# Four small edits ahead of the first layer's convolution output: halo copies, one norm's squares, the sums for a mean, and the start of the modulation columns

## Chip, cores and metric

The kernel runs on one core of one Trainium2 chip. The metric is the device time of one execution in microseconds; the time before is the median of three runs. The profile is that of one execution, with times counted from its span's start. The engines are called as in the profile: PE (matrix products), DVE (vector), ACT (scalar activation), POOL (GpSimd), SP (whose queue issues most transfers).

## The reference, cut to what matters

Sequence 1024, width 1024, two layers, batch 1, everything in float32. Only the first half of layer 0 is touched by the change:

```python
mod = c_act @ ada_w[i] + ada_b[i]
sh_m, sc_m, g_m, sh_f, sc_f, g_f = jnp.split(mod, N_ADA, axis=-1)
h = modulate(rms_norm(x, norm_mix_g[i]), sh_m, sc_m)
u = h @ w1 + b1                       # D -> 2D
a, g = jnp.split(u, 2, axis=-1)
u = a * jax.nn.sigmoid(g)
u = causal_depthwise_conv(u, w_dw, width=31) + b_dw
u = jax.nn.silu(layer_norm(u, ln_g, ln_b))
x = x + (1.0 + g_m) * (u @ w2 + b2)
```

After it come a SwiGLU feed-forward net (width 2816), and in layer 1 a pooling mixer and a second such net, then a last norm.

## The kernel before

The work lies transposed: channels on the 128 partitions, time along the free axis. There are eight channel tiles (`KT`, called k or p) and two chunks of 512 time steps, A and B. A float32 product is made as three products of 512 columns (`products`): every matrix and every activation is split in a high and a low part, and high by high, high by low and low by high are added in one PSUM bank. `matmul` (line 119) is the one place that issues on PE, so all of PE's instructions have line 122; the `Engine` helper issues all of DVE's, ACT's and POOL's, at line 100.

**Order.** PE's instructions run in the order in which the program emits them. The other engines' orders are laid out by a scheduler at build time, from modelled times and priorities, and are then fixed: each engine and each queue runs its list in order and waits at the head of it. What is emitted when is set by a planner: `unit` collects the stages; `run_units` emits them one after the other; `pace()` (called after each fourth k of a product, and at the end of each unit) lets background tasks emit as much as the planner's clocks of PE, DVE and POOL allow. `finish` and `need` force a task to its end before the next unit. A task that says "load", "stats" or "spread" is left alone for 2.5, 2.75 or 1.5 us of the planner's clock.

**Weights.** `load_weight` (line 394) reads a 512 KB tile to a `raw` buffer (three of them) from SP's queue at line 397; ACT makes the high part (line 399) and the negated high part (line 401); a second read of the same tile, issued by POOL at line 403, adds itself to the latter, which gives the low part. There are five buffers for the pair of parts (`W_BUFS`).

**Stages around the change**, in PE's order: the products of the first four channel pairs of chunk A (tiles `first`); `conv_in((A, 4))` and `conv_in((A, 5))`, each 24 products of `a` and 24 of `g`; then pairs 6 and 7 of A and, with the same weights, of B; pairs 0, 1 and 2 of B; the depthwise convolution of channel tile 7 of chunk A as products with diagonal matrices (`pe_taps`, tile `tap`); pairs 3 and 4 of B; the product with w2 for chunk A (`conv_out`, tile `y`).

**Background tasks** beside them:
- `ada_columns` (line 352) makes four of layer 0's six modulation vectors (j = 2 to 5). For each j there are eight steps; each loads a 512 KB tile `adaw` (two buffers, SP's queue, line 132), and PE takes it in a group of four short products into a bank `ada`. After the eighth step `columns_done` copies the bank (ACT), turns it into columns with four tiny products (bank `adac`), and adds the bias. The task is started by the unit `ada_first` (line 1041), ahead of `conv_in((A, 4))`. A unit after `pe_taps` forces it to its end (line 1065); vectors that end after `held` is set wait for `conv_out`.
- `norm_first` (line 1045) is the norm of chunk B: `Squares.add(k)` squares a tile on ACT and adds it on DVE to a sum in a PSUM bank; then mean, reciprocal root (`mean_rsqrt`: products `var`, twelve small DVE instructions, products `rstd`) and modulation to the tiles `hhi`, `hlo`. It is forced to its end ahead of pair 6 of chunk B.
- `Taps` does the other seven channel tiles' depthwise convolution of chunk A: 31 taps each, on DVE (`ca`, sums in the two spare PSUM banks) or on ACT and POOL (`pr`, `pa`), joined at the end.
- `layer_norm_silu(A)` (line 703) adds the eight convolved tiles up on DVE as they are ready (`acc`), makes the `mean` on PE, subtracts it, and goes on to squares, `var`, `rstd` and the tiles `vhi`, `vlo` that `conv_out` needs.

`conv_glu` (line 562) makes u from `a` and `g`, and for chunk A copies u's last 30 columns to `uhalo` on POOL (line 568), from where `conv_u` copies them in front of chunk B's u, on POOL as well. `bank` hands out one of six PSUM banks, `temp` one of four SBUF tiles named t, or one of two named `acc`.

Of the kernel before, what the change touches and what calls it, by code (L numbers as in the profile page):

```python
# [12 lines left out]
AF = mybir.ActivationFunctionType  # L13
ALU = mybir.AluOpType
MUL, ADD, SUB = ALU.mult, ALU.add, ALU.subtract
# [4 lines left out]
KT = D // P  # L20
# [4 lines left out]
HALO = CW - 1  # L25
# [15 lines left out]
FIRST = 4  # L41
# [64 lines left out]
def trunk(ctx, tc, xT, c, vec, ada, adan, w1, w2, wgu, wdn, wpl, out):  # L106
# [3 lines left out]
    V_ = Engine(nc.vector, "V", clock, PRICES["V"], lambda i: order(i))  # L110
    G_ = Engine(nc.gpsimd, "G", clock, PRICES["G"], lambda i: order(i))
    S_ = Engine(nc.scalar, "S", clock, PRICES["S"], lambda i: order(i))
# [11 lines left out]
    def order(ins):  # L124

        if behind[0] and last_mm[0] is not None:
            tc.add_manual_dep(ins.ins, last_mm[0], edge, reason="behind the products")
        return ins
# [29 lines left out]
    def nm(s):  # L158
        uid[0] += 1
        return f"{s}_{uid[0]}"  # L160
# [7 lines left out]
    def step(t, e):  # L168
        behind[0] = not t.urgent
        before = {k: engines[k].spent for k in "VG"}  # L170
        with tc.high_priority(offset=0 if t.urgent else -LATER):
            moved = t.step(e)
        behind[0] = False
        for k in "VG":
            clock[k] += (stretch[0] - 1) * (engines[k].spent - before[k])
        return moved
# [13 lines left out]
    def finish(*these):  # L190
        forced[0] = True
        for t in these:
            while not t.done:
                e = "V" if clock["V"] <= clock["G"] else "G"
                o = "VG"[e == "V"]
                if not any(step(q, e) for q in [t] + tasks) and not any(step(q, o) for q in [t] + tasks):
                    raise RuntimeError("nothing moves")
                clock["PE"] = max(clock["PE"], min(clock["V"], clock["G"]))
        forced[0] = False

    class Task:


        def __init__(self, gen, urgent=False, at=None):
            self.gen, self.done, self.urgent, self.until, self.mark = gen, False, urgent, 0.0, None
            tasks.insert(0 if urgent else len(tasks) if at is None else at, self)
# [31 lines left out]
    def bank(name):  # L238
        return ps.tile([P, 512], F32, tag="mm", name=nm(name))
# [15 lines left out]
    def temp(n, name="t", bufs=0):  # L255
        t = tmp.tile([P, TMPW], F32, tag=name if bufs else "t", name=nm(name), bufs=bufs or 4)
        return t[:, :n]
# [9 lines left out]
    x = [[cst.tile([P, ch.n], F32, name=f"x_{ch.i}_{k}") for k in range(KT)] for ch in chunks]  # L267
# [21 lines left out]
    def V(name, j, n=1):  # L289
        b = _COLS[name] + j  # L290
        return vecs[:, b : b + n]
# [4 lines left out]
    uhalo = cst.tile([P, KT, HALO], F32, name="uhalo")  # L296
# [158 lines left out]
    class Squares:  # L455


        def __init__(self, ch, psum=False):
            self.ch, self.acc, self.psum = ch, None, psum

        def add(self, k):
            ch = self.ch
            if self.acc is None:
                self.acc = bank("acc") if self.psum else temp(ch.n, "acc", 2)
                S_.activation(self.acc, x[ch.i][k], AF.Square)
            else:
                sq = temp(ch.n)
                S_.activation(sq, x[ch.i][k], AF.Square)
                was = self.acc
                if self.psum and k == KT - 1:  # L470
                    self.acc = temp(ch.n, "acc", 2)
                V_.tensor_tensor(self.acc, was, sq, op=ADD)

    def sum_sq(srcs, n):
        acc = None
# [50 lines left out]
    def unit(emit, *weights):  # L526
        units.append((weights, emit))
# [26 lines left out]
    def conv_u(ch, p):  # L554
        u = st["u", ch.i, p] = wslot(ch, "u")
        if ch.i == 0:
            G_.memset(u[:, :HALO], 0.0)
        else:
            G_.tensor_copy(u[:, :HALO], uhalo[:, p, :])
        return u  # L560

    def conv_glu(ch, p, ba, bg):
        u = st["u", ch.i, p]
        sg = temp(ch.n)
        S_.activation(sg, bg, AF.Sigmoid, bias=V("conv_b1", KT + p))
        V_.scalar_tensor_tensor(u[:, HALO:], ba, V("conv_b1", p), sg, op0=ADD, op1=MUL)
        if ch.i == 0:
            G_.tensor_copy(uhalo[:, p, :], u[:, ch.n : ch.n + HALO])

    def conv_in(*todo):  # L570

        def emit(take):
            got = {}
            for each in todo:
                if each is None:
                    finish(T["norm_b"])
                    continue
                ch, p = each
                conv_u(ch, p)
                wts = got.setdefault(p, [])  # L580
                b = [bank("a"), bank("g")]
                for i in range(2):
                    if len(wts) == i:
                        wts.append(take())
                    for k in range(KT):
                        products(b[i], wts[i], k, st["h", ch.i][k], k == 0, k == KT - 1)
                        if k % 4 == 3:
                            pace()
                conv_glu(ch, p, *b)
                if ch.i == 0 and p in PE_TAPS:  # L590
                    split_u(p)
                elif ch.i == 0:
                    T["taps", 0, p] = Taps(A, p)
        tiles = list(dict.fromkeys(e[1] for e in todo if e))
        unit(emit, *[w1[p, i] for p in tiles for i in range(2)])

    def split_u(p):

        u = st["u", 0, p]
        hi, lo = st["us", p] = [wslot(B, name, F32R) for name in ("uhi", "ulo")]  # L600
        S_.copy(hi, u)
        either(A.width).tensor_tensor(lo, u, hi.bitcast(F32), op=SUB)
# [100 lines left out]
    def layer_norm_silu(ch):  # L703

        n = ch.n
        vs = [st["u", ch.i, k][:, HALO:] for k in range(KT)]
        acc = temp(n, "acc", 2)
        for k in range(1, KT):
            while not (st["taps", ch.i][k - 1] and st["taps", ch.i][k]):
                yield "wait"  # L710
            V_.tensor_tensor(acc, vs[0] if k == 1 else acc, vs[k], op=ADD)
            yield
        yield "stats"
        b = bank("mean")
        matmul(b, ones, acc, start=True, stop=True)
        if ch.i == 0:
            yield from centred(vs, b, n)
        else:
            for k in range(KT):
                V_.tensor_tensor(vs[k], vs[k], b, op=SUB)  # L720
                yield
        acc = yield from sum_sq([vs[k] for k in CENTRED], n)
        rstd = yield from mean_rsqrt(acc, n)
        S_.activation(tmp.tile([P, 16], F32, tag="col0", name=nm("col"), bufs=1)[:, 0:1], acc[:, 0:1], AF.Silu)
        hv = [(slot(ch, "vhi"), slot(ch, "vlo")) for _ in range(KT)]
        for k in range(KT):
            V_.tensor_tensor(vs[k], vs[k], rstd, op=MUL)
            sw = temp(n)
            S_.activation(sw, vs[k], AF.Silu, bias=V("conv_ln_b", k), scale=V("conv_ln_g", k))
            hi, lo = hv[k]  # L730
            if ch.i == 0 and k % 2 == 0:
                V_.tensor_copy(hi, sw)
            else:
                S_.copy(hi, sw)
            (either(n) if ch.i else (G_, V_)[k % 2]).tensor_tensor(lo, sw, hi.bitcast(F32), op=SUB)
            yield
        st["v", ch.i] = hv
# [222 lines left out]
    acc = now(sum_sq([x[0][k] for k in range(KT)], A.n))  # L960
# [52 lines left out]
    T = {}  # L1013
# [6 lines left out]
    def need(*names):  # L1020
        unit(lambda take: finish(*(T[n] for n in names)))
# [19 lines left out]
    def ada_first(take):  # L1041
        T["ada", 0] = Task(ada_columns((2, 3, 4, 5)), False, 0)
        T["ada", 0].free = True
    unit(ada_first)
    def norm_first():
        squares = Squares(B, True)
        for k in range(KT):
            squares.add(k)
            yield
        yield from norm(B, 0, False, ("h", 1), squares=squares)  # L1050
    unit(lambda take: T.__setitem__("norm_b", Task(norm_first(), False, 0)))
    taps(A, *range(FIRST))
    for p in range(FIRST, KT - 1 - SHARE):
        conv_in((A, p))
    some = range(KT - 1 - SHARE, KT)
    conv_in(*[(A, p) for p in some], None, *[(B, p) for p in some])
    put("ln_a", lambda: layer_norm_silu(A), True)
# [4 lines left out]
        for u in pe_taps(p):  # L1062
            unit(*u)
    unit(lambda take: held.__setitem__(0, True))
    unit(lambda take: finish(T["ada", 0]))
    unit(lambda take: finish(*(T["taps", 0, p] for p in range(KT) if p not in PE_TAPS)))
    for p in rest[len(rest) - HOLD - HOLD_LN : len(rest) - HOLD]:
        conv_in((B, p))
    need("ln_a")
    sq_a = Squares(A)  # L1070
    conv_out(A, sq_a, lambda take: [now(columns_done(*g)) for g in held_back])
# [49 lines left out]
    fb_, fa_, last = ffn(B, 0, True), ffn(A, 1, True), ffn(B, 1, True, at_end=True)  # L1121
# [51 lines left out]
```

## Time and profile before

| what | value |
|---|---|
| time, median of three runs | 1880.17 us (1877.83 to 1882.66) |
| the profiled execution's own time | 1878.38 us |
| its span | 1876.6 us |
| busy: PE, DVE, ACT, POOL | 1821.7, 971.8, 984.5, 622.2 us |
| mean clock granted to PE | 0.989 |
| PE waits on `adaw` transfers | 10.4 us in 6 waits |

A group's row reads: line, engine, operation, tile written and tiles read, shapes and count; busy time and mean duration in ns; and, behind the second bar, how long the engine stood idle ahead of the group and what ended that. A row of the timeline reads: start, time that it took, engine, line, operation, tiles, count, and in brackets the idle time before it with its releaser. Rows that begin with SPq or POOLq, or that have line 397 or 403, are transfers; their time is that of issuing, not of moving data. PE's matrix products overlap, so its rows show the time of one product (some 0.39 us) while a new one starts every 0.227 us.

### The profile page before, as it was taken

The page shows a single profiled execution, that of the slowest core. Times are in us where ns is not written, and L with a number is a line of the kernel's source. Part 1 is how long each engine was busy: PE and PEld are TensorE (multiplying, and loading weights), DVE is VectorE, ACT ScalarE, POOL GpSimd, SP SyncE. Part 2 cuts the span into 40 slices and gives each one's busy share as a digit, 9 for nine tenths or more (in the row PEclk, how much of TensorE's full clock was granted, in tenths as well). Part 3 has the DMA queues.
Part 4 walks back from the last instruction along what each step waited for, and adds up shares of the span by engine and source line. Part 5 has one row for each costly group of instructions (what it writes and reads, how often), then busy time and mean ns, then how long its engine had stood idle before and what let it go on. Part 6 is the DMA issues. An engine that isn't in the chain of part 4 may idle for free.

```text
span 1876.6 us, 22033 instructions
## 1 busy us (share of the span) xinstructions
PE 1821.7 (97%) x8197; PEld 1481.9 (79%) x8197; DVE 971.8 (52%) x1489; ACT 984.5 (52%) x1304; POOL 622.2 (33%) x668
## 2 busy tenths in 40 slices
PE   6899999999999999999999999999999999999996
PEld 4676678888888887888888888888888888888886
DVE  7699743998876235486533223644432233323225
ACT  3577756866756454554553445645534454443443
POOL 3488621787753211273211111421111111111111
PEclk9999989999999999999999999999999999999998
DMA  8968558899897986999887887878878879788882
GB/s 265 298 185 233 155 114 202 207 230 218 213 233 186 239 217 165 261 266 291 231 204 181 200 197 179 196 180 208 185 181 199 198 174 247 180 206 187 193 185 61
DMA packets 115292, 382.31 MB, mean 204 GB/s; under 512 B 11889, under 2 KB 22257, under 8 KB 115186
## 3 DMA queue, kind: packets, MB, share of 16 engines
q0 software_dynamic: 43488, 158.35, 46.2%
q1 hardware_dynamic: 70544, 221.51, 34.8%
q8 instruction: 64, 1.05, 0.2%
q10 hardware_dynamic: 1154, 1.05, 0.2%
q14 instruction: 42, 0.34, 0.0%
HBM read 376.67 MB, written 4.19 MB: 203 GB/s over the span
## 4 chain that ended last, share of the span: by engine, by line
PE 91%; DVE 4%; DMA 3%; ACT 0%; issue 0%; POOL 0%; SPq 0%; DVEq 0%; ACTq 0%; POOLq 0%
PE dn L122 25%; PE gate L122 25%; PE up L122 24%; PE y L122 6%; PE a L122 3%; PE g L122 3%; PE first L122 2%; DMA adaw<-in_adan_dram 2%; DVE t L100 1%; PE ada L122 1%; PE tap L122 1%; DVE x L100 1%; DVE adaw L100 1%; PE var L122 1%; DMA w<-in_wdn_dram 1%; DVE acc L100 1%
## 5 line engine op out<-in xcount | busy, mean ns | idle before, releaser
L100 ACT CAST w<-raw 128x1024 fp32r<-128x1024 f32 x312 | 326.0, 1045 | 514.8 <-issue 294.4
L122 PE MATMUL dn<-ghi,w 128*128 128x512 f32 (+1 forms) x1440 | 450.0, 389 | 2.2 <-ACT ghi L100 1.2
L122 PE MATMUL up<-hhi,w 128*128 128x512 f32 x1408 | 451.4, 390 | 0.0
L122 PE MATMUL gate<-hhi,w 128*128 128x512 f32 x1408 | 450.9, 390 | 0.0
L403 POOL DMA_DIRECT2D w<-in_wgu_dram x176 | 154.2, 876 | 767.6 <-ACT w L100 750.1
L100 DVE SCALAR_TENSOR_TENSOR x<-dn,gains,x 128x512 f32<-128x512 f32 (+1 forms) x360 | 261.8, 735 | 122.1 <-PE dn L122 121.7
L122 PEld LDWEIGHTS dn<-ghi,w 128*128 128x128 f32 x1440 | 270.4, 189 | 62.0 <-ACT ghi L100 1.6
L100 ACT ACTIVATE w<-raw 128x1024 fp32r<-128x1024 f32 x302 | 318.9, 1056 | 0.0
L100 DVE TENSOR_TENSOR t<-t,up 128x512 f32<-128x512 f32 x88 | 60.4, 686 | 492.4 <-PE up L122 472.0
L122 PEld LDWEIGHTS gate<-hhi,w 128*128 128x128 f32 x1408 | 264.3, 188 | 55.4
L122 PEld LDWEIGHTS up<-hhi,w 128*128 128x128 f32 x1408 | 264.3, 188 | 54.7
L122 PE MATMUL dn<-glo,w 128*128 128x512 f32 (+1 forms) x720 | 280.7, 390 | 1.6 <-POOL glo L100 1.6
L122 PE MATMUL gate<-hlo,w 128*128 128x512 f32 x704 | 274.3, 390 | 1.5 <-DVE hlo L100 1.5
L122 PE MATMUL up<-hlo,w 128*128 128x512 f32 x704 | 273.9, 389 | 0.0
L100 POOL TENSOR_TENSOR pa<-pa,pr 128x512 f32<-128x512 f32 x165 | 231.0, 1486 | 23.0 <-ACT pr L100 20.3
L100 DVE SCALAR_TENSOR_TENSOR ca<-u,vecs,ca 128x512 f32<-128x512 f32 x255 | 176.2, 746 | 0.7
L122 PEld LDWEIGHTS dn<-glo,w 128*128 128x128 f32 x720 | 136.6, 190 | 30.3 <-POOL glo L100 1.9
L122 PEld LDWEIGHTS gate<-hlo,w 128*128 128x128 f32 x704 | 132.1, 188 | 29.8 <-DVE hlo L100 2.3
L122 PEld LDWEIGHTS up<-hlo,w 128*128 128x128 f32 x704 | 132.2, 188 | 27.2
L403 POOL DMA_DIRECT2D w<-in_wdn_dram x88 | 77.9, 885 | 226.5 <-ACT w L100 224.4
L100 ACT ACTIVATE t<-gate 128x512 f32<-128x512 f32 x88 | 52.3, 594 | 161.0 <-PE gate L122 154.4
L100 DVE SCALAR_TENSOR_TENSOR adaw<-adaw,cact 128x1024 f32<-128x1024 f32 x64 | 106.2, 1660 | 36.0 <-DMA adaw<-in_ada_dram 35.8
(134 smaller groups left out, 1792.3 us busy)
## 6 DMA issues: line engine op xcount, KB each, us to landing
raw<-in_wgu_dram SPq DMA_DIRECT2D x176, 512.0 KB, 7.2
w<-in_wgu_dram POOLq DMA_DIRECT2D x176, 512.0 KB, 8.0
raw<-in_wdn_dram SPq DMA_DIRECT2D x88, 512.0 KB, 5.4
w<-in_wdn_dram POOLq DMA_DIRECT2D x88, 512.0 KB, 9.1
adaw<-in_ada_dram SPq DMA_DIRECT2D x48, 512.0 KB, 7.8
raw<-in_w_dram SPq DMA_DIRECT2D x44, 512.0 KB, 6.2
w<-in_w_dram POOLq DMA_DIRECT2D x34, 512.0 KB, 8.1
adaw<-in_adan_dram SPq DMA_DIRECT2D x32, 512.0 KB, 5.3
```

Of the source, the lines that this page charges most:

```text
L100: self.last = self.order(getattr(self.eng, name)(out, *args, **kw))
L122: last_mm[0] = nc.tensor.matmul(out, lhsT, rhs, start=start, stop=stop).ins.name
L403: order(nc.gpsimd.dma_start(low if len(src.shape) == 2 else low.rearrange("p (a b) -> p a b", a=src.shape[1]), src, accum_op=ADD))
```

## The change

1. `conv_glu` copies u's last columns to `uhalo` on DVE, not POOL.
2. `Squares` is cut in two, `square(k)` and `sum`, and `norm_first` squares tile k before it adds tile k-1. Elsewhere `add` does what it did.
3. In `layer_norm_silu` the sums for the mean of chunk A go to a PSUM bank, all but the last, which goes to an SBUF tile; for chunk B they stay in SBUF, the last going to a second tile.
4. `ada_first` moves behind `conv_in((A, 4))`, and the unit that forces the task to its end moves behind pairs 3 and 4 of chunk B.

```diff
-        def add(self, k):
+        def square(self, k):
             ch = self.ch
-            if self.acc is None:
-                self.acc = bank("acc") if self.psum else temp(ch.n, "acc", 2)
-                S_.activation(self.acc, x[ch.i][k], AF.Square)
+            if k == 0:
+                self.acc = sq = bank("acc") if self.psum else temp(ch.n, "acc", 2)
             else:
                 sq = temp(ch.n)
-                S_.activation(sq, x[ch.i][k], AF.Square)
-                was = self.acc
-                if self.psum and k == KT - 1:
-                    self.acc = temp(ch.n, "acc", 2)
-                V_.tensor_tensor(self.acc, was, sq, op=ADD)
+                self.waiting.append(sq)
+            S_.activation(sq, x[ch.i][k], AF.Square)
+
+        def sum(self, last):
+            was = self.acc
+            if self.psum and last:
+                self.acc = temp(self.ch.n, "acc", 2)
+            V_.tensor_tensor(self.acc, was, self.waiting.pop(0), op=ADD)
+
+        def add(self, k):
+            self.square(k)
+            if k:
+                self.sum(k == KT - 1)
...
-            G_.tensor_copy(uhalo[:, p, :], u[:, ch.n : ch.n + HALO])
+            V_.tensor_copy(uhalo[:, p, :], u[:, ch.n : ch.n + HALO])
...
-        acc = temp(n, "acc", 2)
+        acc = None
         for k in range(1, KT):
             while not (st["taps", ch.i][k - 1] and st["taps", ch.i][k]):
                 yield "wait"
-            V_.tensor_tensor(acc, vs[0] if k == 1 else acc, vs[k], op=ADD)
+            was = vs[0] if k == 1 else acc
+            if k == KT - 1 or ch.i and acc is None:
+                acc = temp(n, "acc", 2)
+            elif acc is None:
+                acc = bank("acc")
+            V_.tensor_tensor(acc, was, vs[k], op=ADD)
             yield
...
-    unit(ada_first)
     def norm_first():
         squares = Squares(B, True)
-        for k in range(KT):
-            squares.add(k)
+        for k in range(KT + 1):
+            if k < KT:
+                squares.square(k)
+            if k > 1:
+                squares.sum(k == KT)
             yield
         yield from norm(B, 0, False, ("h", 1), squares=squares)
...
         conv_in((A, p))
+        if p == FIRST:
+            unit(ada_first)
...
-    unit(lambda take: finish(T["ada", 0]))
     unit(lambda take: finish(*(T["taps", 0, p] for p in range(KT) if p not in PE_TAPS)))
     for p in rest[len(rest) - HOLD - HOLD_LN : len(rest) - HOLD]:
         conv_in((B, p))
+    unit(lambda take: finish(T["ada", 0]))
     need("ln_a")
```

More of the change, by code (lines that the diff above doesn't have):

```diff
@@ L458, in __init__ @@
         def __init__(self, ch, psum=False):
-            self.ch, self.acc, self.psum = ch, None, psum
-        def add(self, k):
+            self.ch, self.acc, self.psum, self.waiting = ch, None, psum, []
+        def square(self, k):
             ch = self.ch
-            if self.acc is None:
-                self.acc = bank("acc") if self.psum else temp(ch.n, "acc", 2)
-                S_.activation(self.acc, x[ch.i][k], AF.Square)
+            if k == 0:
+                self.acc = sq = bank("acc") if self.psum else temp(ch.n, "acc", 2)
             else:
                 sq = temp(ch.n)
-                S_.activation(sq, x[ch.i][k], AF.Square)
-                was = self.acc
-                if self.psum and k == KT - 1:
-                    self.acc = temp(ch.n, "acc", 2)
-                V_.tensor_tensor(self.acc, was, sq, op=ADD)
+                self.waiting.append(sq)
[9 more added lines that the diff above has]
+                self.sum(k == KT - 1)
     def sum_sq(srcs, n):
```

## The prediction, made before the result was known

> **What bounds the kernel now.** I read the busy time by stage first, to see where PE stands still.
>
> ```profile
> 70.70:93.30 22.60, 15.89 (x82) 10.28 (x80) 11.47 (x17) 14.29 (x21) 9.51 (x12) 0.85 0.99 270
> ...
> 231.50:254.50 23.00, 16.09 (x52) 12.42 (x52) 12.79 (x29) 11.48 (x16) 7.12 (x9) 0.70 0.55 114
> ...
> 338.30:1829.00 1490.70, 1486.94 (x6572) 1225.81 (x6571) 701.76 (x1036) 758.87 (x941) 441.25 (x471) 1.00 0.85 207
> ```
>
> The second and third columns are the stretch's length and PE's busy time; the third from the right is the granted clock. From 338 us on PE idles 3.8 us in 1491, so an edit ahead of 338 us is worth only what it takes out of PE's gaps ahead of 338 us. Two stretches hold most: 6.7 us at 70.7 to 93.3, 6.9 us at 231.5 to 254.5, each with a lowered clock on top. The table of waits names two of the causes:
>
> ```profile
> PE ada L122 <- DMA adaw<-in_adan_dram: 10.4, 6, 6.0
> ...
> PE mean L122 <- DVE acc L100: 4.7, 1, 4.7
> ```
>
> **The first stretch** is `conv_in((A, 4))`. PE's timeline, and one row of the chain that ended last for the length of 24 products:
>
> ```profile
> 70.73 0.39 PE L122 MATMUL a<-hhi,w 128*128 128x512 f32 x1
> ...
> 73.54 0.64 PE L122 MATMUL ada<-adaw,ccols 128*32 128x256 f32 x8
> ...
> 77.06 0.64 PE L122 MATMUL ada<-adaw,ccols 128*32 128x256 f32 x8
> ...
> 86.62 1.08 PE L122 MATMUL ada<-adaw,ccols 128*32 128x256 f32 x8 [5.97 <-DMA adaw<-in_adan_dram]
> ...
> 92.68 0.64 PE L122 MATMUL ada<-adaw,ccols 128*32 128x256 f32 x8 [0.74 <-DMA adaw<-in_adan_dram]
> 93.25 0.50 PE L122 MATMUL a<-hhi,w 128*128 128x512 f32 x1
> ```
> ```profile
> 258.23 5.44 PE a L122 x24
> ```
>
> A product takes 5.44 / 24 = 0.227 us; from one column group to the next, 73.54 to 77.06, are 3.52 us for 12 products (2.72) and a group, so a group costs 0.80. The pair needs 48 x 0.227 + 4 x 0.80 = 14.1 us and took 93.25 - 70.73 = 22.5. Of the 8.4 lost, 6.7 are the two waits on `adaw`, and 1.7 is the halved clock behind the first (its group took 1.08, not 0.64).
>
> **The second stretch** is the layer norm of chunk A:
>
> ```profile
> 236.20 2.08 PE L122 MATMUL mean<-acc,ones 128*128 128x512 f32 x2 [4.66 <-DVE acc L100]
> ...
> 247.56 1.86 PE L122 MATMUL var<-ones,acc 128*128 128x1 f32 x8 [2.25 <-DVE acc L100]
> 249.29 0.77 PE L122 MATMUL g<-hhi,w 128*128 128x512 f32 x1
> ...
> 254.41 1.05 PE L122 MATMUL rstd<-ident,col 128*128 128x128 f32 x8
> ```
> ```profile
> 248.00:252.00 4.00, 4.00 (x14) 3.42 (x15) 2.01 (x12) 0.86 (x2) 0.67 (x1) 0.50 0.75 181
> ```
>
> PE waits 4.66 us for the sums of the mean and 2.25 for those of the squares; the clock is then 0.50, and the 12 products from 249.29 to 254.41 take 5.1 us, not 2.7: 2.4 more.
>
> **Edit 4, the columns' start.** It takes nothing away: 32 loads, 32 groups. All move behind 48 products, 10.9 us of PE. What else moves is SP's queue. Its rows, POOL's first and last of three additive reads, and the page's queues:
>
> ```profile
> 65.94 0.90 SPq L132 DMA_DIRECT2D adaw<-in_adan_dram  x2
> 71.37 2.80 SPq L397 DMA_DIRECT2D raw<-in_w_dram  x2
> 74.28 2.53 SPq L132 DMA_DIRECT2D adaw<-in_adan_dram  x1
> 76.90 0.46 SPq L397 DMA_DIRECT2D raw<-in_w_dram  x1
> 77.76 0.33 SPq L132 DMA_DIRECT2D adaw<-in_adan_dram  x1
> 80.99 0.33 SPq L397 DMA_DIRECT2D raw<-in_w_dram  x1
> ```
> ```profile
> 71.99 1.04 POOL L403 DMA_DIRECT2D w<-in_w_dram  x1 [0.54 <-issue]
> ...
> 76.82 0.86 POOL L403 DMA_DIRECT2D w<-in_w_dram  x1 [1.33 <-issue]
> ```
> ```profile
> q0 software_dynamic: 43488, 158.35, 46.2%
> q1 hardware_dynamic: 70544, 221.51, 34.8%
> ```
>
> Four `adaw` loads leave the time from 66 to 78 us. By the queues' shares of the 1876.6 us span a 0.524 MB additive read occupies all transfer engines for 0.462 x 1876.6 x 0.524 / 158.35 = 2.87 us, a `raw` or `adaw` for 1.55. Pair 4 then runs without a group, 70.73 to 81.6. The first group comes 12 products later, at 84.3. Its load is tied behind pair 4's last product, so it takes SP's queue behind the four `raw` reads up to 80.99, with the three additive reads before it. From 71.4 on that is 4 x 1.55 + 3 x 2.87 + 1.55 = 16.4 us of transfers: it lands at 87.8. PE waits 3.5 us, and the clock costs 1.7 again: 5.2 in place of 8.4. **Gain 3.2.** Bounds: the load in time (8.4), and a load behind everything with no gain (0). I take the middle since the queue's sum says so. The later `adaw` waits (10.4 - 6.7 = 3.7 us) I leave: the columns still run beside pairs 0 to 2 of chunk B, which read fresh weights.
>
> Behind the waiting group stand the other products of pair 5, and the taps of its u; behind its load in SP's queue, the `raw` reads of pair 7 and later, not wanted for 25 us.
>
> ```profile
> 223.04 0.64 PE L122 MATMUL ada<-adaw,ccols 128*32 128x256 f32 x8 [1.20 <-DMA adaw<-in_adan_dram]
> ```
>
> This is the last column group, at the fifth of seven pauses of `pe_taps`. Four pauses later, two fall in the taps and two in pair 3 of chunk B, ahead of `var`. That wait hangs on DVE's sums, not on PE, so 2 x 0.80 = 1.6 us of its 2.25 are filled: **gain 1.6**. Whether the 0.65 us left still halve the clock no row tells; the ends are 0 and 2.4, and I take half, **1.2**.
>
> On this point the Trainium skill ("TensorE: Matmul & The Clock Gate", Part 1: The HAM clock gate) says that the clock halves after an idle window of some 3.4 us. The rows speak against so long a gap: 2.25 us were enough here. By the page the 2.4 would be saved whole, and the sum would be 1.2 lower.
>
> **Edits 1 to 3** work on DVE and POOL:
>
> ```profile
> L100 POOL COPY uhalo<-u x8: 201/208/471, 69.7 to 140.1; 128x30 f32<-128x30 f32 x8
> ```
> ```profile
> L100 DVE TENSOR_TENSOR acc<-acc,u 128x512 f32<-128x512 f32 x6 | 11.1, 1857 | 0.2
> ...
> L100 DVE TENSOR_TENSOR acc<-acc,t 128x512 f32<-128x512 f32 x7 | 4.9, 697 | 0.6
> ```
> ```profile
> 226.71 1.05 ACT L100 CAST w<-raw 128x1024 fp32r<-128x1024 f32 x1 [3.05 <-PE tap L122]
> ...
> 231.77 1.27 POOL L100 TENSOR_TENSOR pa<-pa,pr 128x512 f32<-128x512 f32 x1
> ...
> 233.07 0.70 DVE L100 TENSOR_TENSOR ca<-pa,ca 128x512 f32<-128x512 f32 x1 [6.87 <-POOL pa L100]
> ```
>
> The sums of the mean take 1857 ns each where another sum of that size takes 697. With one input in PSUM six cost at best 6 x 1.16 = 7.0 us less; at worst nothing. The eight copies cost DVE 0.2 us each if they run as on POOL, 1.6 (the taps stand behind them; the far end is the last rival); the squares ahead take short waits out of DVE's list. None of it reaches PE by itself: the mean's wait ends with a chain that begins on PE. A tap product frees a weight buffer (226.7), ACT makes two weight parts ahead of POOL's last factor, POOL ends at 233.0, and DVE, idle for 6.87 us by then, adds it. DVE being 5 us earlier makes that idle time longer. So I cost edits 1 to 3 at **0**; if that chain weren't there, up to the 4.66 us of the mean's wait would go.
>
> **Sum.** 3.2 + 1.6 + 1.2 = 6.0 us from the profiled execution's 1878.4: **1872.4**. That execution lies 1.8 us under the median of 1880.2.
>
> **Rivals.**
>
> *The column comes in time* (0.18). The scheduler may put the load ahead of a `raw` read, or the reads may run faster without it. Then the 5.2 go too, and perhaps the clock's other 1.2: 1866. Against it: SP's queue would have to reach it before 79 us.
>
> *The waits only move* (0.15). The load lands as late after its need as before, or the two groups don't fall ahead of `var`: 1878.
>
> *The sum's bank* (0.17, the slower side). The running sum now sits in one of six banks from the first sum, near 137 us, to the mean. Products take two per pair, the columns one:
>
> ```profile
> 204.56 0.50 PE L122 MATMUL tap<-uhi,diag 128*128 128x512 f32 x1
> ```
> ```profile
> 202.03 0.73 DVE L100 SCALAR_TENSOR_TENSOR u<-a,vecs,t 128x512 f32<-128x512 f32 x1
> ...
> 213.82 0.75 DVE L100 SCALAR_TENSOR_TENSOR u<-a,vecs,t 128x512 f32<-128x512 f32 x1 [0.42 <-ACT t L100]
> ```
>
> DVE frees pair 1's bank at 202.8 and pair 2's at 214.6, PE wants the taps' bank at 204.6. With the sum, a column's bank and four of two pairs all six are held. If the taps' bank must be pair 2's, PE waits 10.0 us, with the clock's 2.4, and as much clock again if pair 2's second bank waits for 202.8: 14.8 more, 1887. It decides from 12 us on. For it speaks how late DVE is with u; against it that pair 1's banks are free 1.8 us before the taps, if the scheduler picks those.
>
> *The copies are dear* (0.05).
>
> ```profile
> 133.05 1.78 DVE L100 SCALAR_TENSOR_TENSOR hlo<-t,mod,hhi 128x512 fp32r<-128x512 f32 x1
> ```
> ```profile
> 135.61 0.50 PE L122 MATMUL a<-hhi,w 128*128 128x512 f32 x1
> ```
> ```profile
> L100 POOL TENSOR_TENSOR pa<-pa,pr 128x512 f32<-128x512 f32 x165 | 231.0, 1486 | 23.0 <-ACT pr L100 20.3
> ```
>
> If each copy waits for a whole POOL sum, 8 x 1.49 = 11.9 us come on DVE ahead of chunk B's `hlo`. The last `hlo` ends at 134.8 and is needed at 135.6 + 21 x 0.227 = 140.4: 5.6 us are hidden, 6.3 are not: 1878.7. The Trainium skill ("SBUF — State Buffer", Who interferes with whom) has this rule: a DVE copy within SBUF in a two-port mode and a GpSimd instruction lock each other out, whichever starts later waiting; it also says that two SBUF inputs on DVE collide with GpSimd's reads, to which the 1857 ns agree.
>
> **How the numbers follow.** The forecast has 0.45, with its own range of 1867 to 1877. A measurement of this kernel tells some 0.3% from no change: 5.6 us, so faster is under 1874.5 and slower over 1885.8. Faster: 0.33 of the forecast and all of the first rival, 0.51. Slower: 0.15, of the banks. The same: 0.34. The range is 1863 (the first rival, with part of the mean's wait gone too) to 1883; it leaves out most of the banks' case and the far end of the first rival.
>
> **What would show it.** In the changed profile the first `ada` group stands in pair 5, 60 products after 70.73; its wait on `adaw` is 2 to 5 us and the only one over 2. Two `ada` groups lie between `mean` and `var`, and `var` waits under 1 us. The rows `acc<-acc,u` of chunk A take some 0.7 us, and the mean still waits 4 to 5 us on a chain through POOL. A PE wait on DVE's u or ACT's t between 137 and 235 us would be the bank. A mean that waits under 2 us would show edits 1 to 3 worth more than nothing; any PE gap over 3 us after 338 us would be a re-laid order that I did not foresee.

## The result, and the profile after

The changed kernel takes 1894.07 us (median of four runs, 1891.56 to 1898.28) against 1879.0 for the kernel before beside it: a ratio of 1.0079, 95% interval 1.0058 to 1.0100. It is slower by some 15 us, where 6 us less were forecast. The profiled execution took 1894.32 us, with a span of 1892.6.

Its table of waits (engine, tile and what PE waited for; us in all, times, longest):

```profile
PE ada L122 <- DMA adaw<-in_adan_dram: 6.3, 5, 1.9
PE mean L122 <- DVE acc L100: 6.1, 1, 6.1
PE adac L122 <- ACT t L100: 5.8, 1, 5.8
...
PE rstd L122 <- DVE uhalo L100: 2.8, 1, 2.8
PE a L122 <- DMA w<-in_w_dram: 2.5, 1, 2.5
...
PE a L122 <- DVE hlo L100: 2.1, 1, 2.1
```

The wait on `adaw` did shrink, from 10.4 to 6.3 us. But the mean's wait grew from 4.7 to 6.1, and four rows are new: `adac` (the modulation columns), `rstd`, weights, and `hlo`.

The busy time by stage (length, PE, PEld, DVE, ACT, POOL; then PE's clock, DMA share and GB/s):

```profile
280.00:290.00 10.00, 6.33 (x28) 4.89 (x27) 3.88 (x6) 7.40 (x11) 2.48 (x3) 0.99 0.60 134
290.00:300.00 10.00, 7.92 (x28) 6.56 (x29) 0.86 (x2) 2.03 (x4) 1.12 (x2) 0.67 0.88 193
353.00:1829.00 1476.00, 1472.12 (x6505) 1213.61 (x6505) 700.91 (x1034) 753.19 (x934) 442.15 (x468) 1.00 0.85 208
```

In the last row, from the feed-forward net on, PE idles under 4 us, as before: nearly the whole loss is made ahead of it. A new hole lies at 286 to 292 us, in the product with w2, which had none; the clock from 290 to 300 us is 0.67.

PE's timeline has its cause, and where the last columns' groups went:

```profile
244.56 2.05 PE L122 MATMUL mean<-acc,ones 128*128 128x512 f32 x2 [6.10 <-DVE acc L100]
246.54 1.08 PE L122 MATMUL ada<-adaw,ccols 128*32 128x256 f32 x8
...
251.05 0.64 PE L122 MATMUL ada<-adaw,ccols 128*32 128x256 f32 x8
...
254.57 0.64 PE L122 MATMUL ada<-adaw,ccols 128*32 128x256 f32 x8
...
260.72 0.95 PE L122 MATMUL var<-ones,acc 128*128 128x1 f32 x8
...
292.08 1.01 PE L122 MATMUL adac<-quarters,t 128*128 128x4 f32 x4 [5.75 <-ACT t L100]
```

Three groups stand between `mean` and `var`, behind the point at which `held` is set. By the kernel's rule their vector's columns then wait for `conv_out`, and there its four tiny `adac` products stand between the first two and the other six tiles y, and wait 5.75 us for ACT's copy of the bank. ACT's timeline shows why the copy is late:

```profile
285.69 0.69 ACT L100 ACTIVATE t<-y,vecs 128x512 f32<-128x512 f32 x1 [2.57 <-PE y L122]
286.27 1.04 ACT L100 CAST w<-raw 128x1024 fp32r<-128x1024 f32 x1
287.21 1.06 ACT L100 ACTIVATE w<-raw 128x1024 fp32r<-128x1024 f32 x1
288.16 0.68 ACT L100 ACTIVATE t<-y,vecs 128x512 f32<-128x512 f32 x1
288.73 1.04 ACT L100 CAST w<-raw 128x1024 fp32r<-128x1024 f32 x1
289.67 1.06 ACT L100 ACTIVATE w<-raw 128x1024 fp32r<-128x1024 f32 x1
290.63 0.62 ACT L100 ACTIVATE acc<-x 128x512 f32<-128x512 f32 x1
291.15 0.62 ACT L100 ACTIVATE t<-x 128x512 f32<-128x512 f32 x1
291.67 0.36 ACT L100 COPY t<-ada 128x256 f32<-128x256 f32 x1
```

A copy of 0.36 us, with its input ready for 36 us (the last group's row above ends at 255.2), stands last of nine on a list that runs in order: behind two evacuations of y, four weight parts and two squares. PE's wait ends with this copy and with none of those.

The halo copies and the mean's sums on DVE (the first row: min/median/max in ns, first and last start; the second: busy us and mean ns):

```profile
L100 DVE COPY uhalo<-u x8: 180/314/2226, 70.2 to 147.8; 128x30 f32<-128x30 f32 x8
```
```profile
L100 DVE TENSOR_TENSOR acc<-acc,u 128x512 f32<-128x512 f32 x6 | 4.2, 698 | 0.2
```

The sums fell from 1857 to 698 ns, as forecast. The copies took up to 2.2 us.

The new `rstd` row has a cause on DVE too, in an instruction that no edit touches:

```profile
106.04 5.62 DVE L100 TENSOR_SCALAR col<-col 128x4 int32<-128x4 int32 x1
```
```profile
118.88 1.86 PE L122 MATMUL rstd<-ident,col 128*128 128x128 f32 x8 [2.79 <-DVE uhalo L100]
```

This step of the norm of chunk B took 0.17 us in x1 and x2 (below), and 5.62 here, while POOL ran six sums (8.0 us from 106.32 on). The last of the small instructions that make `col` comes late by it, and PE waits 2.8 us for `rstd` (the bracket names the halo copy, which stands right behind that instruction, at 118.69). In x4 it took 4.2 us, and there PE didn't wait for `rstd`. Whether edit 1 brings the two together or chance does, no run here settles.

To read the kernels side by side I use PE's stages, and each kernel's ratio to executions of the kernel before beside it. The stages run from the first product of chunk A's pair 4 (near 71 us) to the first tap product, from there to `mean`, from there to the first y, and from there to the next `a`. Lengths in us, from the start times in PE's timelines, one execution each:

| kernel | to taps | to mean | to y | y | time, ratio to before (95%) |
|---|---|---|---|---|---|
| before | 133.8 | 31.6 | 32.7 | 43.5 | 1 |
| changed | 139.6 | 33.8 | 30.7 | 52.1 | 1.0079 (1.0058 to 1.0100) |
| x1, edits 2 to 4 | 134.2 | 30.4 | 26.9 | 43.5 | 0.9956 (0.9942 to 0.9970) |
| x2, x1 with the price | 136.0 | 33.5 | 31.0 | 52.3 | 1.0059 (1.0043 to 1.0075) |
| x3, changed without the price | 137.5 | 33.2 | 29.8 | 43.5 | 0.9986 (0.9973 to 1.0000) |
| x4, `held` set later | 137.9 | 33.7 | 31.7 | 43.5 | 1.0030 (1.0014 to 1.0045) |
| x5, edit 4 alone | 132.8 | 30.2 | 28.5 | 43.5 | 0.9963 (0.9950 to 0.9977) |
| x6, edits 2 and 3 | 136.4 | 34.1 | 31.3 | 43.5 | 1.0005 (0.9989 to 1.0020) |
| x7, edits 1 to 3 | 142.7 | 29.7 | 28.7 | 43.5 | 1.0014 (1.0003 to 1.0025) |
| x8, halo from PSUM | 137.9 | 32.0 | 28.5 | 43.5 | 0.9998 (0.9985 to 1.0011) |
| x9, x1 with early loads | 130.6 | 29.9 | 28.5 | 43.5 | 0.9954 (0.9936 to 0.9972) |
| x10, copies on both | 133.4 | 30.4 | 26.9 | 43.5 | 0.9978 (0.9964 to 0.9993) |
| x11, start alone | 132.1 | 30.4 | 30.3 | 43.5 | 0.9983 (0.9971 to 0.9996) |
| x12, end alone | 133.7 | 31.8 | 29.2 | 43.6 | 0.9995 (0.9982 to 1.0008) |

Executions of one kernel scatter (x1 from 1868.2 to 1879.0 us), and x6, whose PE order is that of the kernel before, differs from it by 2.6 us in the first stage. So stage differences under 3 us are not read alone; the ratio decides. Stages also hold different numbers of column groups (0.8 us each): ahead of the taps 27 in the kernel before, 26 in x1, x3 and x5, 24 in the changed kernel and x2.

### The profile page after: what moved, and what is told of

The parts are those of the page before. It is cut to its first block, busy times and chain, and to the rows that moved or that the text cites. A ratio compares the mean times of both kernels' runs of the same rounds, so it can differ in the third digit from the quotient of the medians.

```text
span 1892.6 us, 22065 instructions
## 1 busy us (share of the span) xinstructions
PE 1827.1 (97%) x8197; PEld 1484.7 (78%) x8197; DVE 981.4 (52%) x1493; ACT 989.8 (52%) x1310; POOL 627.5 (33%) x664
## 4 chain that ended last, share of the span: by engine, by line
PE 87%; DVE 7%; DMA 3%; issue 1%; ACT 1%; POOL 0%; SPq 0%; DVEq 0%; ACTq 0%; POOLq 0%
PE dn L122 25%; PE gate L122 25%; PE up L122 24%; PE y L122 6%; PE first L122 2%; PE a L122 2%; PE g L122 1%; DVE ca L100 1%; DMA adaw<-in_adan_dram 1%; DVE t L100 1%; DVE hlo L100 1%; PE tap L122 1%; DVE x L100 1%; DMA w<-in_wdn_dram 1%; PE var L122 1%
## 5 line engine op out<-in xcount | busy, mean ns | idle before, releaser
L100 POOL TENSOR_TENSOR pa<-pa,pr 128x512 f32<-128x512 f32 x169 | 237.5, 1496 | 33.3 <-ACT pr L100 30.0
L122 PEld LDWEIGHTS dn<-glo,w 128*128 128x128 f32 x720 | 136.6, 190 | 30.3 <-POOL glo L100 1.9
L122 PEld LDWEIGHTS gate<-hlo,w 128*128 128x128 f32 x704 | 132.1, 188 | 29.8 <-DVE hlo L100 2.3
L403 POOL DMA_DIRECT2D w<-in_wdn_dram x88 | 78.6, 893 | 225.6 <-ACT w L100 223.8
L100 ACT ACTIVATE pr<-u,vecs 128x512 f32<-128x512 f32 x169 | 112.9, 716 | 24.0 <-DVE u L100 11.7
```

Of the source, the lines that this page charges most:

```text
L100: self.last = self.order(getattr(self.eng, name)(out, *args, **kw))
L122: last_mm[0] = nc.tensor.matmul(out, lhsT, rhs, start=start, stop=stop).ins.name
L403: order(nc.gpsimd.dma_start(low if len(src.shape) == 2 else low.rearrange("p (a b) -> p a b", a=src.shape[1]), src, accum_op=ADD))
```

## The experiments

My theory from this profile: edit 1 makes all of the loss, by its place on DVE's list and by something that it does to the order of emission. For the second there is a line to point at. The `Engine` helper (line 98) books each DVE instruction on the planner's DVE clock, a copy of 30 columns at 0.07 + 30 x 0.00104 = 0.10 us (line 76). `columns_done` says "spread" behind ACT's copy, and is then left alone until 1.5 us behind the later of the DVE and the ACT clock (line 220). POOL's clock, on which the copies were booked before, isn't in that line. The rivals: edit 4 itself is dear, or the sum's PSUM bank.

**x1 to x3: place and price of the copies, apart.**

```diff
 x1:
-            V_.tensor_copy(uhalo[:, p, :], u[:, ch.n : ch.n + HALO])
+            G_.tensor_copy(uhalo[:, p, :], u[:, ch.n : ch.n + HALO])
 x2, behind x1's copy, which is booked on no clock:
+            cost = V_.price("tensor_copy", HALO)
+            clock["V"] = max(clock["V"], clock["PE"]) + cost
+            V_.spent += cost
 x3:
-            V_.tensor_copy(uhalo[:, p, :], u[:, ch.n : ch.n + HALO])
+            order(nc.vector.tensor_copy(uhalo[:, p, :], u[:, ch.n : ch.n + HALO]))
```

> The changed kernel with edit 1 undone: the halo copies are issued on POOL again, edits 2 to 4 stay. By the order of PE's instructions the fourth columns' products then fall in pair 3 of chunk B, not in the product with w2. Theory: edit 1 causes all of the loss, in two ways, by its place on DVE's list (some 6 us by pair 0 of chunk B) and by its price on the planner's DVE clock (which pushes the columns past the taps and into the product with w2, some 8.5 us). Both go: 0.996 to 1.001 of the kernel before, no adac wait over 1 us, pair 0 of chunk B starts within 2 us of 162.6. Rival, edit 4 itself is dear (its transfers collide with the weights' reads): 1.004 or more, with the waits still ahead of 150 us. Rival, the sum's PSUM bank: a PE wait between 137 and 245 us stays, 1.003 or more.

> As x1 (halo copies on POOL, edits 2 to 4), but the planner books each copy on its DVE clock, at the price that it has in the changed kernel, and none on its POOL clock. Nothing that an engine executes is added; only the order of emission differs, and it is that of the changed kernel, with the fourth columns' products between the first products with w2. Theory: the wait in the product with w2 comes back (4 to 6 us, ended by ACT's copy t), the lateness ahead of 150 us doesn't: 6 to 10 us over x1, 1.003 to 1.006 of the kernel before. Rival, the copies' time on DVE is what counts: as x1.

> The changed kernel with the halo copies on DVE, but not booked on the planner's DVE clock. PE's order is that of x1. Theory: no adac wait in the product with w2, but the lateness of chunk B's norm ahead of 150 us stays: 4 to 8 us over x1, 1.001 to 1.004 of the kernel before. If only the planner's price counts: as x1. If the wait in the product with w2 has to do with DVE being late, and not with the order: as the changed kernel, 1.008.

x1 is faster than the kernel before: 1872.5 us, 0.9956, just under the range that I had given. Edit 4's rival falls, and the bank's: in x1 PE waits for none of u's banks between 137 and 245 us. With the price and no copy on DVE (x2) the time is 1891.6; with the copy on DVE and no price (x3), 1877.7, under the range too; with both (the changed kernel), 1894.1. So **the price costs 19 us** (x2 less x1; 16 by the changed kernel less x3) and **the place 2.4 to 5.2**. The price is no work at all: in x2 every engine executes what it executes in x1, but for three taps of the convolution that the planner gave to ACT and POOL (169 products and sums in place of 166) instead of DVE (251 in place of 254). Beforehand I had put it at 6 to 10 us and the place at 4 to 8: the price was undersized.

Of x2's 19 us the table places 17.8: 1.8 ahead of the taps (with two groups less, and within the scatter), 3.1 up to the mean, 4.1 up to y, 8.8 in y. The last is the wait on `adac`. In the middle ones, three groups (2.4 us) come behind the mean, and the mean waits longer. POOL has more to do ahead of it: POOL's sums from 60 to 262 us are first x1's and then x2's, and behind them stand PE's rows in x2.

```profile
L100 POOL TENSOR_TENSOR pa<-pa,pr 128x512 f32<-128x512 f32 x76 | 101.5, 1446 | 17.0 <-ACT pr L100 16.1
```
```profile
L100 POOL TENSOR_TENSOR pa<-pa,pr 128x512 f32<-128x512 f32 x79 | 106.8, 1452 | 15.7 <-ACT pr L100 14.4
```
```profile
241.48 2.04 PE L122 MATMUL mean<-acc,ones 128*128 128x512 f32 x2 [6.09 <-DVE acc L100]
...
289.30 1.02 PE L122 MATMUL adac<-quarters,t 128*128 128x4 f32 x4 [5.75 <-ACT t L100]
```

79 sums, not 76, are 5.3 us more on POOL, and the mean waits 6.1 us, not 2.2. That the one makes the other isn't shown, and the count alone doesn't set the wait: with 75 sums (the kernel before) and with 76 (x3) the mean waits 4.7 us. That the price acts like a switch shows in the order in which the program emits PE's products (built only, not run): booked at a quarter, it is that of x1; at a half, that of the changed kernel. With the full price the first two vectors' columns come one pause of PE's (12 products) later than in x1, the third vector's four, and the last three groups fall past the taps.

**x4: the flag later.**

```diff
-    unit(lambda take: held.__setitem__(0, True))
...
     unit(lambda take: finish(T["ada", 0]))
+    unit(lambda take: held.__setitem__(0, True))
```

> The changed kernel with the flag held set behind the unit that forces the columns to their end, so that the last columns are made in pair 4 of chunk B, ahead of the product with w2. Copies on DVE and their price stay. Theory: the wait of 5.75 us in the product with w2 goes, with its half clock, 8 us under the changed kernel, 1.003 to 1.005 of the kernel before; a new wait of up to 2 us of adac on ACT's list in pair 4 may take its place. Rival, the wait only hides another that stands behind it (the evacuation of y on ACT): under 3 us of difference to the changed kernel, 1.006 or more.

1885.0 us, 1.0030: 9 us under the changed kernel. The y stage is back at 43.5 us, and `adac`, now behind `var`, waits for nothing. So the wait in the product with w2, with the low clock behind it, costs its 8.6 us in full and hides no other.

**x5 to x7: the edits apart.** x5 is the kernel before with edit 4's lines alone, x6 with those of edits 2 and 3, x7 with those of 1 to 3.

> The kernel before with edit 4 alone (columns start one pair later, their forced end moves behind pairs 3 and 4). x1, which is edits 2 to 4, took 0.9956 of the kernel before. Theory: edit 4 is the source of that, by PE's order ahead of the layer norm's var, and edits 2 and 3 are worth nothing, as predicted: 0.994 to 0.998. Rival: the shorter sums of the mean (edit 3) shortened the mean's wait from 4.7 to 2.2 us in x1, and edit 4 is worth little: 0.998 to 1.002, with the mean waiting 4 us or more.

> The kernel before with edits 2 and 3 (the norm's squares one tile ahead, the mean's sums in PSUM), halo copies on POOL, columns as before. Theory: nothing, 0.998 to 1.001, the mean waits 4 to 5 us as before, since its wait hangs on a chain through POOL. Rival: the sums do shorten the mean's wait, 0.995 to 0.998, with a mean wait of 1 to 3 us. A PE wait between 137 and 235 us on DVE u or ACT t would be the sum's bank.

> The changed kernel without edit 4. The price of the copies on the planner's DVE clock is there, but the columns start a pair earlier, so they end before the flag is set, and no adac product falls in the product with w2; by PE's order only var and rstd move by half a pair. Theory: the price does harm only with edit 4; what is left is the copies' place on DVE, 3 to 6 us: 1.001 to 1.004 of the kernel before. Rival: the planner's price does its harm alone: 1.006 or more.

Edit 4 alone has x1's gain (0.9963, 1873.1 us). Edits 2 and 3 are worth nothing (1.0005), though the sums take 696 ns there too, and the mean waits 4.7 us as before. Their rows in x6:

```profile
238.03 0.70 DVE L100 TENSOR_TENSOR ca<-pa,ca 128x512 f32<-128x512 f32 x1 [9.34 <-POOL pa L100]
```
```profile
241.17 2.08 PE L122 MATMUL mean<-acc,ones 128*128 128x512 f32 x2 [4.66 <-DVE acc L100]
```

DVE is ready earlier and waits 9.3 us for POOL, where it waited 6.9. Edits 1 to 3 cost little (1.0014): in x7 every column stands in PE's order where it stands in the kernel before, and only `var` and `rstd` come later, `var` by 24 products. That small total is a net one: the stage ahead of the taps is 8.9 us longer than in the kernel before, and some 6 us come back behind it. So the price does its great harm only where the columns start later. The loss belongs to edits 1 and 4 together; edit 1 without edits 2 and 3 was not run.

**x8 and x10: what the place costs.** x8 computes the halo a second time from PSUM; x10 keeps x3's copy and lets POOL copy as well.

```diff
 x8, in place of x3's copy:
+            e = slice(ch.n - HALO, ch.n)
+            order(nc.vector.scalar_tensor_tensor(uhalo[:, p, :], ba[:, e], V("conv_b1", p), sg[:, e], op0=ADD, op1=MUL))
 x10, behind x3's copy:
+            G_.tensor_copy(spare_halo, u[:, ch.n : ch.n + HALO])
```

> As x3 (halo made on DVE, not booked by the planner; PE's order as in x1), but not by a copy: DVE makes the 30 columns a second time from the PSUM bank and the gate, as it makes u. In x3 and the changed kernel the copy within SBUF took up to 1.0 and 2.2 us, beside POOL's sums, where most took 0.2. Theory A, copies and POOL's instructions hold each other up: each of the eight takes under 0.4 us, chunk B's pair 7 starts 1 to 3 us earlier than in x3, 0.996 to 0.998. Theory B, what costs is that POOL's list, without the halo copies, issues the weight reads of pair 5 four us later (75.9 in place of 72.5): as x3, 0.998 to 1.000, with a wait on w of 2 to 3 us in pair 5.

> As x3 (halo copies on DVE, unbooked by the planner), and POOL makes a second copy of the same 30 columns to a tile that nobody reads, booked as in the kernel before. POOL's list is then that of x1, with the weight reads of pair 5 ahead; DVE's list is that of x3. Theory, what the copies cost on DVE (x3 against x1, 0.3%) is POOL's list, which without them issues those reads four us later: as x1, 0.995 to 0.997, with no wait on w in pair 5. Rival, DVE's own time and the meeting of its copies with POOL: as x3, 0.998 to 1.000.

The eight on DVE in x8, in x10 and in x7 (min/median/max in ns):

```profile
L576 DVE SCALAR_TENSOR_TENSOR uhalo<-first,vecs,t x4: 240/240/242, 70.5 to 76.5; 128x30 f32<-128x30 f32 x4
L576 DVE SCALAR_TENSOR_TENSOR uhalo<-a,vecs,t x4: 236/238/243, 98.6 to 143.9; 128x30 f32<-128x30 f32 x4
```
```profile
L576 DVE COPY uhalo<-u x8: 180/1156/2364, 69.4 to 141.0; 128x30 f32<-128x30 f32 x8
```
```profile
L100 DVE COPY uhalo<-u x8: 170/426/4123, 70.1 to 148.5; 128x30 f32<-128x30 f32 x8
```

The copy within SBUF is held up, by as much as 4 us; of the same 30 columns from PSUM all eight take 0.24 us. That agrees with the rule of the Trainium skill ("SBUF — State Buffer", Who interferes with whom) on DVE's copies and GpSimd. But that is not what costs the time: x8 is no faster than x3 (0.9998 and 0.9986), so theory A falls. x10, whose copies are the slowest of all by the median (7.8 us for the eight, 2.3 in x3), has x1's stages and no wait on weights. What x3 and x8 have in common is POOL's list. Its rows in x1 and in x3, and PE's row in x3:

```profile
72.52 1.04 POOL L403 DMA_DIRECT2D w<-in_w_dram  x1 [0.54 <-issue]
...
75.40 0.87 POOL L403 DMA_DIRECT2D w<-in_w_dram  x1 [1.37 <-issue]
```
```profile
75.93 1.96 POOL L403 DMA_DIRECT2D w<-in_w_dram  x2 [5.20 <-ACT pr L100]
```
```profile
85.39 0.73 PE L122 MATMUL a<-hhi,w 128*128 128x512 f32 x2 [2.90 <-DMA w<-in_w_dram]
```

Without the halo copies the scheduler laid POOL's list anew, and the additive weight reads of pair 5 are issued behind a wait of 5.2 us on ACT (x3), some 3.4 us later than the first in x1. The trace of x10 bears theory B out; its time (0.9978) lies between x1's and x3's and between the two ranges that I had given, and its interval overlaps both. So B is likely, and not settled by time.

**x9, x11, x12: edit 4 in parts.** x9 issues the first two column loads ahead of pair 4 and hands them to the task, which starts behind it as in x1; x11 has only the moved start, x12 only the moved end.

> As x1 (halo copies on POOL, edits 2 to 4), but the first two column tiles are loaded ahead of pair 4, as in the kernel before; the products with them start one pair later, as in x1, and PE's order is that of x1. In x1 the first two loads stand at 75.3 us in SP's queue, the third lands at 98.5 after 12.9 us, and PE waits 6.5 us for it; the transfer engines are full from 81 on, and nearly idle for some 4 us around 74. Theory: the wait is one of transfer time, and two transfers of 1.55 us less behind 75 us shorten it by 3 us: 2 to 4 us under x1, 0.994 to 0.9955 of the kernel before. Rival: the wait is set by the two buffers alone (a load starts only when a group has freed one), so the time is that of x1, 0.9956.

> The kernel before with the first half of edit 4 alone: the columns start one pair later, but are forced to their end ahead of pairs 3 and 4. Theory: the start is worth 0 to 3 us, since the wait on adaw of 6 us only moves from pair 4 to pair 5; mean's wait is 2.2 us as in x5, var's wait stays at 2 us with the half clock behind it: 0.997 to 0.9995 of the kernel before. Rival: the start brings all of edit 4's gain: 0.9963.

> The kernel before with the second half of edit 4 alone: the columns start as before, the unit that forces their end stands behind pairs 3 and 4. By PE's order the only difference is behind the mean: the last adac products and the products var stand 12 matrix products later. Theory: var's wait of 2.25 us and its half clock of 2.4 us go, the mean waits 4.7 us as before: 3 to 5 us, 0.9973 to 0.9985. Rival: the order behind the mean changes nothing, since var waits for DVE wherever it stands and the rstd behind it as well: 1.000.

PE's rows of x1, x9, x11 and x12, in this order:

```profile
98.56 1.08 PE L122 MATMUL ada<-adaw,ccols 128*32 128x256 f32 x8 [6.51 <-DMA adaw<-in_adan_dram]
...
235.82 1.12 PE L122 MATMUL mean<-acc,ones 128*128 128x512 f32 x2 [2.18 <-DVE acc L100]
...
248.17 0.95 PE L122 MATMUL var<-ones,acc 128*128 128x1 f32 x8
```
```profile
94.03 0.64 PE L122 MATMUL ada<-adaw,ccols 128*32 128x256 f32 x8 [1.85 <-DMA adaw<-in_adan_dram]
...
100.20 0.64 PE L122 MATMUL ada<-adaw,ccols 128*32 128x256 f32 x8 [1.00 <-DMA adaw<-in_adan_dram]
```
```profile
234.36 1.12 PE L122 MATMUL mean<-acc,ones 128*128 128x512 f32 x2 [2.17 <-DVE acc L100]
...
244.77 1.05 PE L122 MATMUL var<-ones,acc 128*128 128x1 f32 x8 [1.79 <-DVE acc L100]
```
```profile
236.58 2.08 PE L122 MATMUL mean<-acc,ones 128*128 128x512 f32 x2 [4.66 <-DVE acc L100]
...
251.26 0.95 PE L122 MATMUL var<-ones,acc 128*128 128x1 f32 x8
```

The start alone goes with a shorter wait of the mean (4.66 to 2.17) and leaves most of var's (1.79); the end alone takes var's wait and leaves the mean's. PE's order alone doesn't set the mean's wait: x3 and x8 have x1's order, and there it is 4.7. By time the start is worth 0.9983; the end's 0.9995 can't be told from nothing, where I had expected 3 to 5 us. In x9 the 6.5 us become 1.85 + 1.00, as the transfer theory had it, and the stage ahead of the taps is 3.6 us shorter than in x1. Its time, 1870.4 us, is the lowest of all, but its interval covers x1's. Both beat both kernels; which of the two is better stays open.

## Why the prediction was wrong

- **Edits 1 to 3 at 0: the step that failed.** It priced the copies by what an engine does (0.2 us each, hidden) and left out what the program's planner does with a DVE instruction. Together with edit 4 the price cost 19 us (x2 against x1), and the place 2 to 5; they made a loss of 15 us out of edit 4's gain. For edits 2 and 3 the 0 was right (x6), and so was the reason: a faster DVE doesn't help a mean that waits for POOL.
- **The column groups of edit 4, second half.** The prediction counted pauses, four later, and found two groups in the taps and two ahead of `var`. With edit 1's price the taps hold five groups, as before, and three stand ahead of `var`. The prediction saw groups pass the unit that sets `held` and counted only what they fill; it did not follow their vector to `conv_out`, where the wait costs 8.6 us (x4). In x5, without the price, the last group comes one pause later than in the kernel before, not four, and all groups end in the taps.
- **The gain of 3.2 us in pair 5.** The queue's sum put the first load late. In the changed kernel and in x1 the first two loads went out at 75.3 us, ahead of two `raw` reads at 78.6, and the first two groups didn't wait. The third did: by 6.5 us in x1 and x5, with the clock halved behind it, and by 1.9 in the changed kernel, where PE had already waited 2.5 us for weights. So the wait moved, which was a rival's mechanism. To the taps x5 needs 1.0 us less than the kernel before, with one group (0.8) less.
- **The gain of 2.8 us behind the mean** was there, larger and by another way: in x5 4.2 us from mean to y, where `var` itself stands 24 products later and no longer waits, and 1.4 up to the mean, whose wait fell to 2.2. No group fills the gap ahead of `var`.
- So for edit 4 alone the sum, 1872.4, meets what x5 measured (1873.1) by luck, with its terms wrong one by one. A total that fits is no proof of its terms.
- **Rivals.** In the changed kernel the bank made PE wait nowhere; the one wait of that kind between 137 and 235 us is 0.8 us, in x2. The copies are held up: the eight take 5.7 us in all, where 11.9 were put on them, and x8 and x10 speak against that as the cost. The columns come nearly in time with earlier loads (x9). The kernel lost by a mechanism that I had not named.

## What to carry to other kernels

Where a program plans its own order, an edit's first cost is what it does to the planner's clocks: look up which clock each operation is booked on and who waits for that clock, before its engine time is counted. When work moves past a flag or a stage's end, follow its last instruction to where it comes out, and read what stands ahead of it on that engine's list there. Try edits apart and together; here edits 1 to 3 without edit 4 cost 0.14%, edit 4 without them gained 0.37%, and all four lost 0.79%.

## What the runs showed that was not expected

The halved clock behind a short wait is not a matter of the wait's length alone. PE waited 2.18 us for the mean in x1 and 2.17 in x5, with the same order of products. The stretches around the mean are x1's and then x5's (the third number from the right is the clock):

```profile
235.00:237.00 2.00, 1.18 (x3) 0.68 (x4) 0.69 (x1) 1.28 (x3) 0.33 (x1) 1.00 0.84 164
237.00:239.00 2.00, 2.00 (x10) 1.63 (x9) 1.40 (x3) 1.22 (x3) 1.89 (x3) 1.00 0.92 258
```
```profile
233.00:235.00 2.00, 1.21 (x3) 0.69 (x3) 0.69 (x1) 1.23 (x2) 0.36 (x1) 0.70 0.67 131
235.00:237.00 2.00, 2.00 (x6) 1.19 (x5) 0.48 (x1) 0.59 (x1) 0.93 (x2) 0.50 0.89 258
```

The one keeps its clock, the other runs at half for some 3 us, a difference of about 1.5 us. Edits 2 and 3, which x1 has and x5 has not, don't make it: x9 has them, waited 2.17 us and ran at 0.50 behind it. The Trainium skill ("TensorE: Matmul & The Clock Gate", Part 1: The HAM clock gate) calls the window by which the clock is set free-running; a wait that meets it well or badly would look like this. The gaps here are shorter than the 3.4 us that it gives for a window.
